# A two-layer streaming encoder on one core: the last stage's buffers split over two pools, the first opened earlier, and two scheduling orders dropped

## The chip, the cores and the metric

The kernel runs on one core of one Trainium2 chip. The metric is the device time of one execution, in microseconds (us). A core has TensorE (PE in the profile), VectorE (DVE), ScalarE (ACT), GpSimd (POOL) and SyncE (SP). Here nearly all transfers are issued from SP's queue, a few from ACT's. Each engine carries out its own instructions in program order and waits on semaphores for those of others.

## The reference

`x` is 1024 x 1024 float32 (frames by features). Two layers with residuals, each `x + mixer(rmsnorm(x))`, then a last rmsnorm. Layer 0:

```python
u_s5, g_s5, q, k, v, g_ret = split(h @ w_in)
y = gelu(s5_scan(u_s5))                       # diagonal state space, chunks of 64 frames
y_s5 = y * sigmoid(y @ glu_w + glu_b) * silu(g_s5)
q, k = rope(q) * 64**-0.5, rope(k)            # 8 heads, 64 wide; v 128 wide
y_ret = retention(q, k, v) * silu(g_ret)      # scores within chunks, a decayed state across
x = x + concat(y_s5, y_ret) @ w_out
```

Layer 1 is a Conformer convolution: `a, b, g = split(h @ w_in)`, `a * sigmoid(b)`, a causal depthwise convolution 31 frames wide, a layer norm, silu, a gate `silu(g)`, and an output projection.

## The kernel before

**Products.** A float32 operand is held as two halves that TensorE takes in a fast format: `h` (the value rounded) and `l` (value minus `h`). Each product is three matmuls, `h*h`, `h*l`, `l*h`. A `CAST` that makes an `h` and a subtraction that makes an `l` therefore stand ahead of every operand. Weights come by `wload_pieces` (`wf_X` from memory, `wh_X` on ACT, `wl_X` on POOL).

**Stages.** In time: projections and scan of layer 0 (to about 315 us), retention in four pairs of heads (pair 0 to 3, to about 545 us), the GLU product `y @ glu_w` (`mm_glu`, about 528 to 620 us, so it begins inside pair 3), the output projection, layer 1.

**Retention, one pair.** `ret_proj` makes q and k (`mm_q`, `mm_k`; `qraw` and `kraw` are evicted copies, `qswp` and `kswp` their halves swapped by small DMAs, `qrot` and `krot` the rotated results). Rope's table for q, 1 MB, comes as `ropeq_<pair>`. `ret_heads` makes transposed keys `kt` (from PE's `ktp`), the state products `kv` and the states `S`, the scores (`sp` on PE, masked on DVE into `sc`), and the outputs `ro`; then a norm and a gate `grl_<head>`, stored to memory as `yr_d`.

**y_pass.** In each pair two row blocks of the scan's output, `cb = k` and `k + 4`, are loaded (`yp_<cb>` from `y_d`), passed through gelu on ACT into `yn_<cb>` and stored to `yn_d`. DVE then makes four sums and differences of the two blocks (the GLU product is done with seven products of quarter size instead of eight) and splits the results: `th0_k` and `th1_k` are the `h` parts, `yn` is overwritten by the `l` part, and both are stored to `t_d`. The function is a generator; the caller runs it part by part (`next(parts)`). The pool tags `yp` (one buffer, shared by `yp_*` and `th*`) and `ynt` (two buffers) lie in pool `retq`, with rope's tables, `qraw`, `gs` and others. In pair 2 the store of `yn_6` goes out on ACT's queue; all other stores of this kind are on SP's.

**GLU operands.** `y_quarter` loads quarters of `yn_d` (`y11f`, `y21f`, `y22f`) and splits them. `load_split` reads quarters of `t_d` (`yt1h`, `yt2h`, ...). `gated` loads `yg` and `yn<nb>_<h>` (nb 0 to 3) for the gate behind the product, in pool `l1`; `gu` are copies of partial products. `gs`, stored to `ws_d`, are sums of the GLU's weights for the seven products.

**Order.** A scheduler simulates the kernel's instructions and writes each engine's order. It is steered by priorities, by buffers becoming free, by `issue_after(x)` (what is inside comes after x) and by `self.order(late, first)` (late is placed after first, where the engine would otherwise be free to choose). A pool's space is reused only when the earlier pool is closed; `early.close()` closes `retq` and pool `l1` (all of the last stage's buffers) is opened in its place. In pair 3, `turned()` is called behind the code for q's last addition (`qadds`, the sum that makes `qrot`).

Of the kernel before, what the change touches and what calls it, by code (L numbers as in the profile page):

```python
# [19 lines left out]
P = 128  # L20
# [51 lines left out]
class Trunk:  # L72
# [898 lines left out]
    def y_pass(self, rp, k):  # L971


        nc = self.nc
        yns = []
        for i, cb in enumerate((k, k + 4)):
            yt = rp.tile([P, 8, P], F32, name=f"yp_{cb}", tag="yp", bufs=1)
            self.wdma[f"yp{cb}"] = nc.sync.dma_start(yt[:], self.y_d[cb].rearrange("i h g m -> (h g) i m"))
            yn = rp.tile([P, P, 8], F32, name=f"yn_{cb}", tag="ynt", bufs=2)

            behind = {(2, 0): self.third_v, (2, 1): self.last_v, (3, 1): self.third_v}.get((k, i)) if k > 1 else None
            with self.tc.issue_after(behind.ins) if behind else nullcontext():
                nc.scalar.activation(yn[:], yt[:].rearrange("p i m -> p m i"), AF.Gelu_apprx_tanh)
            yn = yn[:].rearrange("p m i -> p (m i)")
            (nc.scalar if (k, i) == (2, 1) else nc.sync).dma_start(self.yn_d[cb * P:(cb + 1) * P], yn)
            yns.append(yn)
        (b11, b12), (b21, b22) = ((y[:, :HALF], y[:, HALF:]) for y in yns)
        v = nc.vector
        yield
        with self.tc.issue_after(self.last_raw.ins):  # L990
            v.tensor_tensor(b22, b22, b12, op=ALU.subtract)
            v.tensor_tensor(b12, b12, b11, op=ALU.subtract)
            v.tensor_tensor(b11, b22, b11, op=ALU.add)
            v.tensor_tensor(b21, b11, b21, op=ALU.subtract)
        yield
        for i in range(2):
            hi = rp.tile([P, T], F32R, name=f"th{i}_{k}", tag="yp", bufs=1)
            v.tensor_copy(hi[:], yns[i])
            if (k, i) == (1, 0):
                yield  # L1000
            v.tensor_tensor(yns[i].bitcast(F32R), yns[i], hi[:].bitcast(F32), op=ALU.subtract)
            self.wdma[f"th{i}_{k}"] = nc.sync.dma_start(self.t_d[i, 0, k * P:(k + 1) * P], hi[:].bitcast(F32))
            nc.sync.dma_start(self.t_d[i, 1, k * P:(k + 1) * P], yns[i])

    def glu_sums(self, g, tag):
# [5 lines left out]
        for i in range(2):  # L1011
            nc.sync.dma_start(q[i], self.A["w_glu"][i, m, :, :, c].rearrange("p j k n -> p j (k n)"))
        (a11, a12), (a21, a22) = ((t[:, 0, :], t[:, 1, :]) for t in q)
# [6 lines left out]
        with self.tc.issue_after(self.last_swap.ins):  # L1020
            for i in range(2):
                nc.sync.dma_start(self.ws_d[i, m, :, :, c].rearrange("p j k n -> p j (k n)"), q[i])

    def retention(self, st):
        nc, A = self.nc, self.A
        rp = self.rp = self.pool("ret", 1, stack=st)
        early = ExitStack()
        rq = self.rq = self.pool("retq", 1, stack=early, side="right")
        self.rk = rq.tile([P, 2, T], F32, name="ropek")
        nc.sync.dma_start(self.rk[:], A["rope_k"])  # L1030
# [3 lines left out]
        for pair in range(4):  # L1034
# [145 lines left out]
    def ret_heads(self, pair, K, Q, qadds, mask, kdec, V, turned, scored):  # L1180
# [12 lines left out]

        with self.tc.issue_after(self.last_kt.ins):
            for add in qadds:
                add()
# [113 lines left out]
    def layer0_back_and_layer1(self, st):  # L1310
# [55 lines left out]
        def gated(nb, h, z, turned=False):  # L1366
            yg = lp.tile([P, HALF], F32, name=f"yg{nb}_{h}", tag="u", bufs=5)
            nc.sync.dma_start(yg[:], self.gs_d[rows(nb), hs(h)])
            yn = lp.tile([P, HALF], F32, name=f"yn{nb}_{h}", tag="ev", bufs=3)
            nc.sync.dma_start(yn[:], self.yn_d[rows(nb), hs(h)])  # L1370
            times = lambda: gp.tensor_tensor(yg[:], yg[:], yn[:], op=ALU.mult)
# [632 lines left out]
```

## Time and profile before

| | |
|---|---|
| runs | 1134.13, 1137.13, 1139.33 us; median 1137.13 us |
| profiled execution | 1139.25 us, span 1137.5 us |
| busy | PE 1121.5 us (99%), DVE 854.2, POOL 645.7, ACT 496.3 |
| granted TensorE clock | near full in 39 of 40 slices |
| memory traffic | 261.46 MB, 230 GB/s mean |

The profile is that of one execution. Span is first to last instruction; what lies around it is 1139.25 - 1137.5 = 1.75 us. PE's busy time counts pipelined matmuls, so a 99% busy PE may still be slowed by short waits and by its clock. A row such as `484.38 2.07 PE L1254 MATMUL ro<-S,qrot ... x14 [3.06 <-DVE sc L1231]` says: 14 instructions from 484.38 us on, together 2.07 us, ahead of which PE stood idle for 3.06 us, ended by DVE's `sc` of line 1231.

### The profile page before, as it was taken

Reading aid. Unit: us, or ns where it says so; the run is one execution under the profiler, and the core shown is the slowest. Engines: PE = TensorE matmul, PEld = TensorE weight load, DVE = VectorE, ACT = ScalarE, POOL = GpSimd, SP = SyncE. Lnnn points to the kernel's source line nnn. Section 1 sums busy time; section 2 is a strip of 40 time slices with the busy share of each in tenths; the row PEclk is TensorE's granted clock in tenths of the full one; section 3 lists DMA queues with packets and bytes.
Section 4 is the critical chain, followed back from the end, with each engine's and each line's share of the span. In section 5 each row is a group of like instructions: output and inputs, shape, how many; then the busy total and the mean of one; then the engine's idle time right before and its main releaser. Section 6 shows DMA issues by size and latency. Waiting matters only on the chain.

```text
span 1137.5 us, 17227 instructions
## 1 busy us (share of the span) xinstructions
PE 1121.5 (99%) x6286; PEld 982.4 (86%) x6286; DVE 854.2 (75%) x1473; ACT 496.3 (44%) x729; POOL 645.7 (57%) x440
## 2 busy tenths in 40 slices
PE   9999999999999999999999999999999999999997
PEld 8888888888888889889888888888888888888876
DVE  7975798888418468476779633599999899999754
ACT  7323232232232231324446524546535676346673
POOL 2059999999246264341541110589544468678843
PEclk9999999999999999989999999999999999999999
DMA  9444365455397776767999988666678655358964
GB/s 346 131 140 145 116 207 179 172 175 182 114 305 280 246 225 199 273 208 256 379 367 320 357 317 279 204 221 205 239 254 295 237 183 173 112 171 265 320 229 167
DMA packets 118069, 261.46 MB, mean 230 GB/s; under 512 B 10720, under 2 KB 42464, under 8 KB 117344
## 3 DMA queue, kind: packets, MB, share of 16 engines
q1 hardware_dynamic: 114240, 247.22, 64.2%
q10 hardware_dynamic: 3744, 13.14, 3.0%
q8 instruction: 49, 0.80, 0.3%
q14 instruction: 36, 0.29, 0.1%
HBM read 181.48 MB, written 74.65 MB: 225 GB/s over the span
## 4 chain that ended last, share of the span: by engine, by line
PE 71%; DMA 9%; DVE 7%; POOL 6%; issue 3%; ACT 3%; SPq 1%; POOLq 0%; ACTq 0%; DVEq 0%
PE mm_g L213 10%; PE mm_wo L213 9%; PE mm_g L210 5%; PE mm_b L213 5%; PE mm_wo L210 5%; PE mm_a L213 5%; PE mm_u L213 3%; PE mm_oc L213 3%; PE mm_b L210 2%; PE mm_a L210 2%; PE mm_q L213 2%; PE mm_k L213 2%; PE mm_u L210 2%; PE y L962 1%; PE mm_oc L210 1%
## 5 line engine op out<-in xcount | busy, mean ns | idle before, releaser
L1604 DVE SCALAR_TENSOR_TENSOR cv<-u,convw,cv 128x512 f32<-128x512 f32 x390 | 268.3, 749 | 10.6 <-ACT cv L1570 8.5
L1564 POOL TENSOR_TENSOR tp<-tp,tp 128x512 f32<-128x512 f32 x64 | 83.0, 1297 | 33.8 <-ACT tp L1563 32.8
L210 PE MATMUL mm_g<-xh,wh_g 128*128 128x512 f32 x256 | 98.9, 386 | 0.0
L213 PE MATMUL mm_g<-xl,wh_g 128*128 128x512 f32 x256 | 97.3, 380 | 0.0
L213 PE MATMUL mm_g<-xh,wl_g 128*128 128x512 f32 x256 | 97.2, 380 | 0.0
L454 POOL TENSOR_TENSOR s1q<-s1q,s1q 128x512 f32<-128x512 f32 x12 | 17.6, 1465 | 89.8 <-ACT s1q L449 89.8
L1563 ACT ACTIVATE tp<-u,convw 128x512 f32<-128x512 f32 x64 | 45.4, 718 | 33.6 <-POOL tp L1564 32.7
L200 POOL TENSOR_TENSOR wl_glu<-wf_glu,wh_glu 128x1024 fp32r<-128x1024 f32 x14 | 34.3, 2455 | 42.1 <-ACT wh_glu L197 37.8
L210 PEld LDWEIGHTS mm_g<-xh,wh_g 128*128 128x128 f32 x256 | 48.4, 189 | 8.6 <-issue 1.2
L213 PEld LDWEIGHTS mm_g<-xh,wl_g 128*128 128x128 f32 x256 | 48.4, 189 | 6.9
L213 PEld LDWEIGHTS mm_g<-xl,wh_g 128*128 128x128 f32 x256 | 48.4, 189 | 6.7 <-issue 0.4
L200 POOL TENSOR_TENSOR wl_v<-wf_v,wh_v 128x1024 fp32r<-128x1024 f32 x12 | 31.3, 2608 | 37.2 <-ACT wh_v L197 37.1
L210 PE MATMUL mm_oc<-zh,wh_woc 128*128 128x512 f32 (+1 forms) x144 | 51.0, 365 | 1.2 <-ACT zh L1306 1.1
L213 PE MATMUL mm_oc<-zh,wl_woc 128*128 128x512 f32 (+1 forms) x144 | 51.3, 357 | 0.5 <-POOL wl_woc L200 0.5
L213 PE MATMUL mm_oc<-zl,wh_woc 128*128 128x512 f32 (+1 forms) x144 | 51.3, 357 | 0.0
L210 PE MATMUL mm_g<-h1h,wh_cg 128*128 128x512 f32 x128 | 48.9, 382 | 0.0
L210 PE MATMUL mm_wo<-ysh,wh_wos 128*128 128x512 f32 x128 | 48.9, 382 | 0.0
L213 PE MATMUL mm_b<-h1l,wh_cb 128*128 128x512 f32 x128 | 48.7, 381 | 0.1
L213 PE MATMUL mm_u<-xl,wh_u 128*128 128x512 f32 x128 | 48.6, 380 | 0.0
L213 PE MATMUL mm_b<-h1h,wl_cb 128*128 128x512 f32 x128 | 48.6, 380 | 0.0
L213 PE MATMUL mm_wo<-ysl,wh_wos 128*128 128x512 f32 x128 | 48.5, 379 | 0.0
L213 PE MATMUL mm_wo<-ysh,wl_wos 128*128 128x512 f32 x128 | 48.5, 379 | 0.0
(538 smaller groups left out, 3622.5 us busy)
## 6 DMA issues: line engine op xcount, KB each, us to landing
wf_g<-w_ab SPq DMA_DIRECT2D x16, 512.0 KB
wf_wos<-w_out SPq DMA_DIRECT2D x16, 512.0 KB
wf_wor<-w_out SPq DMA_DIRECT2D x16, 512.0 KB
wf_cb<-w_c SPq DMA_DIRECT2D x16, 512.0 KB
wf_ca<-w_c SPq DMA_DIRECT2D x16, 512.0 KB
wf_woc<-w_out_c SPq DMA_DIRECT2D x16, 512.0 KB
wf_v<-w_v SPq DMA_DIRECT2D x12, 512.0 KB
wf_cg<-w_c SPq DMA_DIRECT2D x11, 512.0 KB
```

The source lines that it names most:

```text
L200: self.low_made = self.lows[name] = lo[i].tensor_tensor(wl[:].rearrange(fl)[:, c], wf[:, c], h.bitcast(F32), op=ALU.subtract)
L210: nc.tensor.matmul(ps, wh[:, kb, :], xh, start=start, stop=False, **more)
L213: self.last_mm = nc.tensor.matmul(ps, a[:, kb, :], b, start=False, stop=stop and i == 1, **more)
L454: nc.gpsimd.tensor_tensor(a, a, sq[:], op=ALU.add)
L962: yield nc.tensor.matmul(ps[g2][:, cols(q)], W3[r, c, q, :], S[r, c, q, :], start=False, stop=q == 3 and c == 1)
L1563: nc.scalar.mul(sk[:], u[:, k:k + HALF], cw[:, nb, k:k + 1])
L1564: gp.tensor_tensor(s0[:], s0[:], sk[:], op=ALU.add)
L1604: v.scalar_tensor_tensor(dst[:], *tap, accs_[i][:], op0=ALU.mult, op1=ALU.add)
```

## The change

No operation is added or removed; every engine has as many instructions as before. What changes is where buffers lie and what the scheduler may put where:

1. `yp`, `ynt` and `th` move from `retq` into a pool of their own, `rety`.
2. In pair 3, `turned()` closes `retq` directly behind q's last addition and opens pool `l1a` in its place (tags `u`, `ev`, `tp`, `cq`, `cs`, `pilot`, `sq`; `yg` is tag `u`, `yn<nb>_<h>` tag `ev`). Then `y_pass`'s last part is run, `rety` closed and pool `l1b` opened for the other tags. Class `Two` picks the pool by tag.
3. In pair 3 q's last addition is no longer held behind `kt`, and y's last split (`th0_3`, `th1_3`) no longer behind the last of the `y11l` splits. Instead the first `y11l` split is put after `th0_3`'s low part.
4. Of five hand-made orders of DMAs four go: `y212` after `th0_3`, `yt200` after `th0_3`, `ropeq3` after `yp6`, `grl5` after `glu1`. The one of `yt100` after `glu9` stays.

```diff
+class Two:
+    FIRST = ("u", "ev", "tp", "cq", "cs", "pilot", "sq")
...
+    def tile(self, *args, tag=None, **kw):
+        pool = self.first if tag in self.FIRST else self.rest
+        return pool.tile(*args, **kw, **({"tag": tag} if tag else {}))
...
-            v.tensor_tensor(yns[i].bitcast(F32R), yns[i], hi[:].bitcast(F32), op=ALU.subtract)
+            low = v.tensor_tensor(yns[i].bitcast(F32R), yns[i], hi[:].bitcast(F32), op=ALU.subtract)
+            if (k, i) == (3, 0):
+                self.order(self.y_first, low)
...
         rq = self.rq = self.pool("retq", 1, stack=early, side="right")
+        sums = ExitStack()
+        ry = self.pool("rety", 1, stack=sums)
...
-                parts = self.y_pass(rq, pair)
+                parts = self.y_pass(ry, pair)
...
             def turned():
                 if pair == 3:
-                    with self.tc.issue_after(self.y_low.ins):
-                        next(parts, None)
                     early.close()
-                    self.lp = self.pool("l1", side="right")
+                    first = self.pool("l1a", side="right")
+                    next(parts, None)
+                    sums.close()
+                    self.lp = Two(first, self.pool("l1b", side="right"))
...
-        with self.tc.issue_after(self.last_kt.ins):
+        with self.tc.issue_after(self.last_kt.ins) if pair < 3 else nullcontext():
             for add in qadds:
                 add()
         turned()
...
+            if i == 0:
+                self.y_first = self.y_low
...
-        for late, first in (('y212', 'th0_3'), ('yt200', 'th0_3'), ('ropeq3', 'yp6'), ('grl5', 'glu1'), ('yt100', 'glu9')):
+        for late, first in (('yt100', 'glu9'),):
             self.order(self.wdma[late], self.wdma[first])
```

The remaining edits only store handles of DMAs in `wdma`. Lines of the changed file are 13 to 20 higher than before.

What it does to the order of instructions is seen at three places. First SP's queue between pairs 2 and 3. The rows before, from the load of weight `gs1_3` on:

```order
L1012 DMA gs1_3_4388<-w_glu 128x2x512
L1022 DMA ws_d_110<-gs1_3_4388 256x1x512
L985 DMA yn_d_91<-yn_2_4620 128x1024
L1288 DMA yr_d_92<-grl_3_4162 128x1024
L978 DMA yp_6_4623<-y_d_87 128x8x128
L1288 DMA yr_d_92<-grl_2_4160 128x1024
L1086 DMA ropeq_3_4845<-rope_q 128x2048
L1022 DMA ws_d_110<-gs0_3_4387 256x1x512
L1242 DMA grl_4_4695<-gr_d_90 128x1024
L193 DMA wf_glu0_4987<-w_glu 128x1024
L193 DMA wf_glu1_4993<-w_glu 128x1024
L1242 DMA grl_5_4697<-gr_d_90 128x1024
```

and after:

```order
L1027 DMA gs1_3_4391<-w_glu 128x2x512
L1104 DMA ropeq_3_4848<-rope_q 128x2048
L1037 DMA ws_d_110<-gs1_3_4391 256x1x512
L998 DMA yn_d_91<-yn_2_4623 128x1024
L1306 DMA yr_d_92<-grl_3_4165 128x1024
L991 DMA yp_6_4626<-y_d_87 128x8x128
L1306 DMA yr_d_92<-grl_2_4163 128x1024
L1037 DMA ws_d_110<-gs0_3_4390 256x1x512
L1260 DMA grl_4_4698<-gr_d_90 128x1024
L1260 DMA grl_5_4700<-gr_d_90 128x1024
L206 DMA wf_glu0_4990<-w_glu 128x1024
L206 DMA wf_glu1_4996<-w_glu 128x1024
```

`ropeq_3` has moved from behind the second `yr_d` store to directly behind `gs1_3`, and `grl_5` from behind the two `wf_glu` loads to in front of them.

The second place is SP's queue in pair 3, from the store of `yn_7` on. Before:

```order
L985 DMA yn_d_91<-yn_7_5215 128x1024
L1298 DMA y21f0_5473<-yn_d_91 128x512 x2
L1298 DMA y21f2_5484<-yn_d_91 128x512
L1002 DMA t_d_93<-th0_3_5259 128x1024
L1298 DMA y21f2_5484<-yn_d_91 128x512
L1343 DMA yt2h0_5511<-t_d_93 128x512
L1003 DMA t_d_93<-yn_3_5210 128x1024
```

and after:

```order
L998 DMA yn_d_91<-yn_7_5218 128x1024
L1388 DMA yg0_0_5578<-gs_d_89 128x512
L1390 DMA yn0_0_5580<-yn_d_91 128x512
L1390 DMA yn1_0_5605<-yn_d_91 128x512
L1390 DMA yn2_0_5679<-yn_d_91 128x512
L1345 DMA y22f0_5853<-yn_d_91 128x512
L1345 DMA y22f1_5859<-yn_d_91 128x512
L1345 DMA y22f2_5865<-yn_d_91 128x512
L1390 DMA yn3_0_5703<-yn_d_91 128x512
L1017 DMA t_d_93<-th0_3_5266 128x1024
L1018 DMA t_d_93<-yn_3_5213 128x1024
L1316 DMA y21f0_5480<-yn_d_91 128x512 x2
```

Eight loads of 256 KB, which were issued later before, now stand between the store of `yn_7` and that of `th0_3`; the four `y21f` loads come behind the stores of `th0_3` and its low part. `yn3_0` waits for a buffer of `yn0_0`, which POOL's product of `yg0_0` and `yn0_0` frees.

The third place is DVE at the same time (`CAST th` makes an `h` part, the row below it the low part). Before:

```order
L991 TENSOR_TENSOR yn_7_5215<-yn_7_5215,yn_3_5210 128x512
...
L1308 TENSOR_TENSOR y11l0_5225<-y11f0_5222,y11h0_5224 128x512
L1308 TENSOR_TENSOR y11l1_5230<-y11f0_5222,y11h1_5229 128x512
L1308 TENSOR_TENSOR y11l2_5236<-y11f2_5233,y11h2_5235 128x512
L1308 TENSOR_TENSOR y11l3_5241<-y11f2_5233,y11h3_5240 128x512
L998 CAST th0_3_5259<-yn_3_5210 128x1024
L1001 TENSOR_TENSOR yn_3_5210<-yn_3_5210,th0_3_5259 128x1024
L1191 TENSOR_TENSOR kt_3_5244<-ktp0_3_5245,kdec_3_4843 128x512
L1191 TENSOR_TENSOR kt_3_5244<-ktp1_3_5251,kdec_3_4843 128x512
L1112 TENSOR_TENSOR qrot_3_4978<-qrot_3_4978,qswp_3_4977 128x512 x2
L998 CAST th1_3_5264<-yn_7_5215 128x1024
```

and after:

```order
L1130 TENSOR_TENSOR qrot_3_4981<-qrot_3_4981,qswp_3_4980 128x512 x2
L1004 TENSOR_TENSOR yn_7_5218<-yn_7_5218,yn_3_5213 128x512
...
L1011 CAST th0_3_5266<-yn_3_5213 128x1024
L1014 TENSOR_TENSOR yn_3_5213<-yn_3_5213,th0_3_5266 128x1024
L1328 TENSOR_TENSOR y11l0_5228<-y11f0_5225,y11h0_5227 128x512
L1328 TENSOR_TENSOR y11l1_5233<-y11f0_5225,y11h1_5232 128x512
L1328 TENSOR_TENSOR y11l2_5239<-y11f2_5236,y11h2_5238 128x512
L1328 TENSOR_TENSOR y11l3_5244<-y11f2_5236,y11h3_5243 128x512
L1011 CAST th1_3_5271<-yn_7_5218 128x1024
L1014 TENSOR_TENSOR yn_7_5218<-yn_7_5218,th1_3_5271 128x1024
L1209 TENSOR_TENSOR kt_3_5247<-ktp0_3_5248,kdec_3_4846 128x512
L1209 TENSOR_TENSOR kt_3_5247<-ktp1_3_5254,kdec_3_4846 128x512
```

`qrot_3` is now ahead of y's four sums, `th0_3` and its low part ahead of the `y11l` splits, and `kt` behind `th1_3` and its low part.

More of the change, by code (lines that the diff above doesn't have):

```diff
@@ L58, with __init__ @@
 V_NG0, V_NG1, V_FG, V_GLUB, V_CB, V_LNG, V_LNB = range(7)
+class Two:
+    FIRST = ("u", "ev", "tp", "cq", "cs", "pilot", "sq")
+    def __init__(self, first, rest):
+        self.first, self.rest = first, rest
+    def tile(self, *args, tag=None, **kw):
+        pool = self.first if tag in self.FIRST else self.rest
+        return pool.tile(*args, **kw, **({"tag": tag} if tag else {}))
 class Halves:
@@ L984, in y_pass @@
             yn = yn[:].rearrange("p m i -> p (m i)")
-            (nc.scalar if (k, i) == (2, 1) else nc.sync).dma_start(self.yn_d[cb * P:(cb + 1) * P], yn)
+            self.wdma[f"y{cb}"] = (nc.scalar if (k, i) == (2, 1) else nc.sync).dma_start(self.yn_d[cb * P:(cb + 1) * P], yn)
             yns.append(yn)
@@ L1000, in y_pass @@
                 yield
[L1001 removed]
+            low = v.tensor_tensor(yns[i].bitcast(F32R), yns[i], hi[:].bitcast(F32), op=ALU.subtract)
+            if (k, i) == (3, 0):
+                self.order(self.y_first, low)
             self.wdma[f"th{i}_{k}"] = nc.sync.dma_start(self.t_d[i, 0, k * P:(k + 1) * P], hi[:].bitcast(F32))
[L1003 removed]
+            self.wdma[f"tl{i}_{k}"] = nc.sync.dma_start(self.t_d[i, 1, k * P:(k + 1) * P], yns[i])
     def glu_sums(self, g, tag):
@@ L1011, in glu_sums @@
         for i in range(2):
-            nc.sync.dma_start(q[i], self.A["w_glu"][i, m, :, :, c].rearrange("p j k n -> p j (k n)"))
+            self.wdma[f"gs{i}_{g}"] = nc.sync.dma_start(q[i], self.A["w_glu"][i, m, :, :, c].rearrange("p j k n -> p j (k n)"))
         (a11, a12), (a21, a22) = ((t[:, 0, :], t[:, 1, :]) for t in q)
@@ L1021, in glu_sums @@
             for i in range(2):
-                nc.sync.dma_start(self.ws_d[i, m, :, :, c].rearrange("p j k n -> p j (k n)"), q[i])
+                self.wdma[f"ws{i}_{g}"] = nc.sync.dma_start(self.ws_d[i, m, :, :, c].rearrange("p j k n -> p j (k n)"), q[i])
     def retention(self, st):
@@ L1367, in gated @@
             yg = lp.tile([P, HALF], F32, name=f"yg{nb}_{h}", tag="u", bufs=5)
-            nc.sync.dma_start(yg[:], self.gs_d[rows(nb), hs(h)])
+            self.wdma[f"yg{nb}_{h}"] = nc.sync.dma_start(yg[:], self.gs_d[rows(nb), hs(h)])
             yn = lp.tile([P, HALF], F32, name=f"yn{nb}_{h}", tag="ev", bufs=3)
-            nc.sync.dma_start(yn[:], self.yn_d[rows(nb), hs(h)])
+            self.wdma[f"yn{nb}_{h}"] = nc.sync.dma_start(yn[:], self.yn_d[rows(nb), hs(h)])
             times = lambda: gp.tensor_tensor(yg[:], yg[:], yn[:], op=ALU.mult)
```

2 lines of the change are left out of this document (1 added, 1 removed).

## The prediction

> **What bounds the kernel now.** First the page for the busy shares: PE carries the kernel from end to end, so only three things can move the time: PE's waits, its clock, and an operand that becomes late. I read PE's waits next (which line stood, who released it, us in total, times, longest):
>
> ```profile
> PEclk9999999999999999989999999999999999999999
> PE ro L1254 <- DVE sc L1231: 3.1, 1, 3.1
> PE mm_glu L210 <- ACT wh_glu L197: 1.4, 1, 1.4
> ...
> PE mm_glu L210 <- DVE mm_gluz L1447: 0.6, 1, 0.6
> ```
>
> The longest wait of all, 3.1 us on `ro`, lies where the change moves SP's queue, the second and the 0.6 us one in the GLU stage behind the other moves; and the one slice with a clock digit below 9 holds the first of them. So I read the chain that ended that wait, PE's timeline around it with the same stage of the next pair beside it, and three short windows (PE, PEld, DVE, ACT, POOL busy, clock, DMA share, GB/s):
>
> ```profile
> 464.18 6.71 DMA yp<-y_d
> ...
> 473.01 7.06 DMA yn_d<-yn
> ...
> 480.77 0.68 DVE kraw L1096
> ...
> 482.09 1.63 DVE yn L993
> ```
> ```profile
> 484.38 2.07 PE L1254 MATMUL ro<-S,qrot 64*128 64x128 f32 x14 [3.06 <-DVE sc L1231]
> 486.38 3.78 PE L1259 MATMUL ro<-v,sc 128*128 128x128 f32 x16
> 489.81 0.75 PE L210 MATMUL mm_k<-xh,wh_k 128*128 128x512 f32 x1
> 490.38 0.40 PE L213 MATMUL mm_k<-xl,wh_k 128*128 128x512 f32 x1
> ...
> 540.69 1.16 PE L1254 MATMUL ro<-S,qrot 64*128 64x128 f32 x16
> 541.78 2.05 PE L1259 MATMUL ro<-v,sc 128*128 128x128 f32 x16
> 543.59 0.46 PE L210 MATMUL mm_glu<-y21h,wh_glu 128*128 128x512 f32 x1
> ```
> ```profile
> 460.00:462.00 2.00, 2.00 (x20) 2.00 (x19) 1.56 (x4) 0.47 (x1) 0.00 (x0) 1.00 0.01 2
> 476.00:478.00 2.00, 2.00 (x22) 1.59 (x22) 0.85 (x2) 0.00 (x0) 0.35 (x1) 1.00 1.02 410
> 484.00:486.00 2.00, 1.62 (x13) 1.62 (x14) 2.00 (x4) 0.00 (x0) 0.00 (x0) 0.50 0.00 0
> 556.00:558.00 2.00, 1.52 (x7) 1.22 (x8) 2.00 (x5) 1.58 (x3) 1.88 (x2) 1.00 1.04 390
> ```
>
> The chain reads: `yp_6` is loaded, gelu makes `yn_6`, its store (on ACT's queue) starts at 473.01 and takes 7.06 us; only then may DVE overwrite `yn_6` with y's sums, and behind those stands `sc`, for which PE waits until 484.38. Behind the wait the clock is 0.50: the 14 + 16 `ro` matmuls up to 489.81 take 5.43 us, while the 32 of pair 3 take 543.59 - 540.69 = 2.90 us at full clock, that is 2.72 for 30. The wait has a second bill, about 5.43 - 2.72 = 2.7 us, and 490.38 - 489.81 = 0.57 instead of 0.22 us for the first `mm_k`, so 2.9 us in round numbers. Behind the 1.4 us wait (window 556 to 558) the clock stayed at 1.00. And the DMA engines, full at 410 GB/s while the store waits its turn, moved 2 GB/s at 460 to 462.
>
> **The change part by part.**
>
> *Rope's table for pair 3 goes ahead, `grl_5` too.* The issues and what they wait for:
>
> ```profile
> 456.42 0.63 SPq L1012 DMA_DIRECT2D gs<-w_glu  x1
> 462.01 0.59 SPq L1022 DMA_DIRECT2D ws_d<-gs  x1
> ...
> 466.90 0.51 SPq L1086 DMA_DIRECT2D ropeq<-rope_q  x1
> ...
> 469.73 6.99 SPq L193 DMA_DIRECT2D wf_glu<-w_glu  x2
> 476.83 0.36 SPq L1242 DMA_DIRECT2D grl<-gr_d  x1
> ```
> ```profile
> 456.49 2.52 POOL L1111 TENSOR_TENSOR qswp<-qswp,ropeq 128x512 f32<-128x512 f32 x2 [7.34 <-DMA qswp<-qraw]
> ```
>
> `ropeq_3` is now next after the load at 456.42, but its buffer is free only when POOL has read the old table, at 456.49 + 2.52 = 459.0. SP stands there from 457.1 until 459.0; the next row behind it was issued only at 462.0, so this wait delays nobody. The transfer of 1 MB then runs from 459.0 to about 461.6 (at 410 GB/s) in a stretch with idle DMA engines, instead of among the transfers in front of the `yn_6` store: 2.6 us of their work is gone. Against it, `grl_5` (0.5 MB, 1.3 us at that rate) now is ahead of the `wf_glu` loads, so among those in front. If the store comes out behind everything issued earlier it lands 1.3 us sooner with `grl_5` fully counted, 2.6 without. Bounds: 0 (the store on its own queue never waited for SP's) and 2.6. I take 1.8, between the two cases. Every us goes through: sums, `sc`, `ro` hang on that store. *First term: -1.8.* What is late next is `kraw`, which DVE does between the sums; it needs only `mm_k`, done before the wait.
>
> *The clock.* The wait then is 3.06 - 1.8 = 1.3 us, about as long as the 1.4 us behind which the clock stayed at 1.00. I take the half clock as gone: *second term: -2.9.* Bounds 0 and -2.9; the nearest row is the 1.4 us wait.
>
> [...]
>
> *Eight loads of 256 KB go ahead in pair 3; `y21f` and the stores of `th0_3` follow.* The stage in two windows, then the rows of SP and DVE:
>
> ```profile
> 520.00:530.00 10.00, 10.00 (x85) 9.82 (x84) 8.75 (x13) 5.82 (x11) 2.35 (x1) 1.00 0.43 128
> 530.00:540.00 10.00, 10.00 (x101) 8.56 (x100) 8.63 (x17) 2.23 (x4) 0.07 (x1) 1.00 1.01 338
> ```
> ```profile
> 516.86 0.32 SPq L985 DMA_DIRECT2D yn_d<-yn  x1
> ...
> 526.61 0.32 SPq L1002 DMA_DIRECT2D t_d<-th  x1
> ```
> ```profile
> 520.70 0.69 DVE L991 TENSOR_TENSOR yn<-yn,yn 128x512 f32<-128x512 f32 x1 [11.01 <-ACT v L1146]
> ...
> 523.48 2.50 DVE L1308 TENSOR_TENSOR y11l<-y11f,y11h 128x512 fp32r<-128x512 f32 x4
> ...
> 526.61 1.23 DVE L1001 TENSOR_TENSOR yn<-yn,th 128x1024 fp32r<-128x1024 f32 x1
> 528.26 1.29 DVE L1191 TENSOR_TENSOR kt<-ktp,kdec 128x512 f32<-128x512 f32 x2 [0.42 <-PE ktp L1189]
> ...
> 532.02 0.69 DVE L998 CAST th<-yn 128x1024 fp32r<-128x1024 f32 x1 [0.80 <-DMA t_d<-th]
> ```
> ```profile
> 528.71 0.38 PE L213 MATMUL mm_glu<-y11l,wh_glu 128*128 128x512 f32 x1
> ...
> 533.12 1.75 PE L1208 MATMUL kv<-v,kt 128*64 128x128 f32 x28
> ```
>
> From 520 to 530 the DMA engines were busy 0.43 of the time, from 530 on always: 5.7 us of idle transfer time, room for the 2 MB that move ahead (5.2 us at 390 GB/s). Everything behind them, the weights `wf_glu` included, then comes some us earlier. What that is worth is read from the two waits.
>
> ```profile
> 551.84 1.05 ACT L197 CAST wh_glu<-wf_glu 128x1024 fp32r<-128x1024 f32 x1 [0.80 <-DMA wf_glu<-w_glu]
> ...
> 554.83 0.67 ACT L1382 ACTIVATE sg<-mm_glu,hgb 128x512 f32<-128x512 f32 x1
> 555.40 1.03 ACT L197 CAST wh_glu<-wf_glu 128x1024 fp32r<-128x1024 f32 x1
> ```
> ```profile
> 588.08 1.05 ACT L197 CAST wh_glu<-wf_glu 128x1024 fp32r<-128x1024 f32 x1 [6.38 <-DMA wf_glu<-ws_d]
> ```
>
> The 1.4 us wait at 556.5 is for the `wh_glu` cast at 555.40, which ACT reached late: 0.80 us because it stood for a load at 551.84, and 0.57 us for the second `sg` ahead of it, which now is behind it. Together 1.37; I take *third term: -1.2*, bounds 0 (the load is not earlier) and -1.4. At 588.08 ACT again stood for a weight load, for 6.38 us, and DVE's `mm_gluz`, for which PE waits 0.6 us, is at the end of that chain. *Fourth term: -0.8*: the 0.6 us and as much again in the small delays of matmuls around it, cut by half; bounds 0 and -1.7.
>
> What these moves put at risk, each with its cover:
> - `y11l` comes behind `th0_3` and its low part, 0.69 + 1.23 = 1.9 us later, done at 527.9 instead of 526.0. PE takes the first at 528.71: cover 0.8 us, cost 0. Without it, PE's `mm_glu` waits as much.
> - `kt` now comes behind `th1_3`, which waits for the store of `th0_3` (they share a buffer). SP issues that store behind `yn3_0`, and `yn3_0` behind POOL's product. A 512 KB store out of a quiet stretch took 520.70 - 516.86 = 3.8 us, so `yg0_0` and `yn0_0` are there by about 522, POOL's product (2.52 / 2 = 1.3 us each for that size) by 523.4. `th0_3` is cast by 524.2 (the sums start at 520.70 as before and take 2.8 us). Issued at 524.3 its store lands between 528.1 (3.8 us) and 529.7 (5.4 us, as 526.61 to 532.02); then 0.69 + 1.23 + 1.29 us make `kt` at 531.3 to 532.9. PE wants it at 533.12: cover 0.2 to 1.8 us, cost 0.
> - `qrot` ahead of the sums falls into DVE's 11.01 us of idle time. Cost 0.
> - `y21f` is issued behind the stores of `th0_3`, some 2 us later, and ACT's casts come with it; PE takes the first `y21h` only at 543.59, some 15 us after those loads can land. Cost 0.
> - The pools only fix addresses; tags in `l1b` come free at the same event as before. Cost 0.
>
> *Sum:* -1.8 - 2.9 - 1.2 - 0.8 = -6.7 us, against the profiled execution's 1139.25: 1132.55. That execution is 2.1 us above the median of the runs shown (1137.13), which gives 1130.4. Since the terms lie nearer to their upper bounds than to 0, I take 1131.5.
>
> **The rivals.**
> - *The store does not care.* It is alone on ACT's queue, so it may have had its share of the engines whatever SP queued: `grl_5` and `wf_glu` still fill the engines when it comes. Then the first two terms are 0 and -2.0 is left: 1135.1. For it: the two queues are separate. Against it: 0.5 MB in 7.06 us is 74 GB/s out of 410, less than a fifth; a fair half would have been done in 2.6 us and a start.
>   [...]
> - *The clock halves all the same.* 1.3 us of waiting and what lies around it may be enough, or the wait shrinks by less. Then -1.8 - 2.0 = -3.8: 1133.3.
> - *The GLU stage gives its gain back.* Later `y21f`, ACT's other order, and a full DMA stretch that merely begins sooner: the third and fourth terms are 0: -4.7, 1132.4.
> - *Slower.* `th0_3`'s store is held up by `yn3_0`. If the eight loads slow one another and `yn0_0` lands as late as `yp` did in a full stretch (6.71 us), POOL is done at 525.9, the store lands at 529.7 to 531.3, `kt` is made at 532.9 to 534.5. Every us past 533.1 is one of PE's, with `kv`, `S` and `sc` behind it. It decides when the store lands after 529.9. At the worst the second cast stands as long again (some 4 us) and the wait of 3 to 4 us halves the clock as at 484: +3.9 + 2.9 = +6.8, with no gain in pair 2 to set against it 1143.9; with it (-4.7) about 1139.2.
>
> **How the numbers follow.** The forecast (both regions gain, full clock) has a chance of 0.47, the store's rival 0.14, the half clock 0.14, the GLU rival 0.12, the slower one 0.13. The range 1127.0 to 1138.0: below, all four terms at their bounds (-2.6 - 2.9 - 1.4 - 1.7 = -8.6 from the median: 1128.5) and 1.5 for the scatter of a median; above, the store's rival and the better part of the slower one. The likeliest case's own range is 1128 to 1133.5. What a measurement of this kernel can tell from no change is about 0.5%, 5.7 us: faster means under 1131.4, where somewhat over half of the forecast lies, with parts of the half clock's and the GLU rival's, and gains that I don't see: 0.42; slower (over 1142.8) only the worst end of the slower case: 0.08; the rest, 0.50, is no change that can be told.
>
> **What would show it.** In the changed kernel's trace: `ropeq` issued near 459 and the DMA engines busy from 459 to 462; the `yn_d` store on ACT's queue at 5 to 6 us instead of 7.06; the wait in front of `ro` at 1 to 1.5 us and no window at clock 0.50 around 485; DMA share well over 0.43 from 520 to 530; `th0_3`'s store issued by 524.5, `kt` ready ahead of PE's `kv`; no 1.4 us wait on `wh_glu`. The prediction is wrong if the store still takes 7 us, if a new wait of PE appears at `kv` or at `y11l`, or if the clock falls at another place.

## The result and the profile after

The changed kernel takes 1141.14 us (median of 14 runs, 1138.59 to 1144.31), the kernel before 1137.70 (14 runs, 1133.45 to 1140.74): ratio 1.0037, 95% interval 1.0025 to 1.0049. It is slower by some 4 us, where some 6 us faster (1131.5) was forecast. The profiled execution took 1141.18 us with a span of 1139.4, against 1139.25 and 1137.5 before. All rows below are of such single executions.

First PE's waits of the changed kernel, to be laid beside those that the prediction shows (line that stood, who released it, us in total, times, longest):

```profile
PE ro L1272 <- DVE sc L1249: 2.4, 1, 2.4
PE mm_glu L223 <- ACT sg L1402: 1.9, 1, 1.9
PE mm_glu L223 <- ACT mm_glus L1402: 1.3, 1, 1.3
...
PE mm_glu L226 <- DVE y11l L1328: 0.4, 1, 0.4
```

The wait on `ro` has shrunk from 3.1 to 2.4 us, not to 1.3. The wait of 1.4 us in the GLU stage is now one of 1.9. The 0.6 us on `mm_gluz` are gone, and in their place stand 1.3 us on `mm_glus` and 0.4 on `y11l`.

Where the time goes is seen in PE's timeline at three milestones: the last `mm_q` of pair 3, the first matmul on `yt2`, the first `mm_wo` of the stage that follows. Before:

```profile
505.09 0.38 PE L213 MATMUL mm_q<-xh,wl_q 128*128 128x512 f32 x1
...
556.48 0.48 PE L210 MATMUL mm_glu<-yt2h,wh_glu 128*128 128x512 f32 x1 [1.41 <-ACT wh_glu L197]
...
613.28 0.38 PE L210 MATMUL mm_wo<-ysh,wh_wos 128*128 128x512 f32 x1
```

and after, with the two waits between:

```profile
484.38 2.07 PE L1272 MATMUL ro<-S,qrot 64*128 64x128 f32 x14 [2.36 <-DVE sc L1249]
...
505.33 0.38 PE L226 MATMUL mm_q<-xh,wl_q 128*128 128x512 f32 x1
...
530.85 0.48 PE L226 MATMUL mm_glu<-y11l,wh_glu 128*128 128x512 f32 x1 [0.44 <-DVE y11l L1328]
...
557.93 0.48 PE L223 MATMUL mm_glu<-yt2h,wh_glu 128*128 128x512 f32 x1 [1.92 <-ACT sg L1402]
559.58 0.63 PE L226 MATMUL mm_glu<-y21l,wh_glu 128*128 128x512 f32 x1
...
611.36 0.48 PE L223 MATMUL mm_glu<-yt1h,wh_glu 128*128 128x512 f32 x1 [1.34 <-ACT mm_glus L1402]
...
616.64 0.38 PE L223 MATMUL mm_wo<-ysh,wh_wos 128*128 128x512 f32 x1
```

`ro` starts at 484.38 in both kernels, and `mm_q` ends 0.24 us apart: between pairs 2 and 3 the change brought nothing. From there to `mm_wo` it was 613.28 - 505.09 = 108.19 us and is 616.64 - 505.33 = 111.31. The loss of 3.1 us lies in the GLU stage. The windows say why the matmuls around 559.58 take 0.63 us each (PE, PEld, DVE, ACT, POOL busy, clock, DMA share, GB/s):

```profile
484.00:486.00 2.00, 1.62 (x13) 1.62 (x14) 2.00 (x4) 0.00 (x0) 0.00 (x0) 0.52 0.00 0
520.00:530.00 10.00, 10.00 (x86) 9.87 (x86) 8.89 (x9) 5.01 (x9) 3.47 (x2) 1.00 0.88 304
555.00:560.00 5.00, 3.08 (x12) 2.19 (x11) 3.32 (x7) 4.78 (x7) 4.62 (x3) 0.92 0.36 121
558.00:562.00 4.00, 4.00 (x12) 3.17 (x13) 1.79 (x4) 1.79 (x3) 4.00 (x4) 0.65 0.87 275
```

The clock is still halved at 484 to 486 and now also behind the 1.92 us wait: the 4 us at 0.65 lose 4 x 0.35 = 1.4 us, and since it is at 0.50 from 559.16 to 562.57, 3.41 us, it is 1.7 us in all. The account of the stage is then 0.44 (`y11l`) + 0.51 (1.92 for 1.41) + 1.7 (clock) + 1.34 (at 611) - 0.6 (the one gone) = 3.4 us, a little more than the 3.1 measured. Behind 616 the two executions differ by 1.4 us the other way, which is less than the runs of one kernel scatter. That the stage itself is longer is no accident of one execution: in the next part's two runs it is 608.66 - 502.61 = 106.05 us (e1, the kernel before but for two orders) and 613.80 - 502.09 = 111.71 us (e3, the changed kernel but for the same two).

The eight loads do fill the idle stretch (share 0.88 from 520 to 530, before 0.43). But the idle time comes back: 0.36 from 555 to 560, where before the engines were full. The bytes were moved, and the weights behind them came no sooner.

**Why PE waits at 558 and 611.** First the two weight loads on SP's queue before:

```profile
531.87 0.42 SPq L193 DMA_DIRECT2D wf_glu<-w_glu  x1
...
545.61 0.33 SPq L193 DMA_DIRECT2D wf_glu<-w_glu  x1
```

and SP's queue, then ACT and DVE, of the changed kernel:

```profile
525.02 0.32 SPq L1390 DMA_DIRECT2D yn<-yn_d  x1
525.58 0.32 SPq L1017 DMA_DIRECT2D t_d<-th  x1
...
531.42 0.32 SPq L1316 DMA_DIRECT2D y21f<-yn_d  x1
...
537.00 0.64 SPq L206 DMA_DIRECT2D wf_glu<-w_glu  x1
...
546.79 0.33 SPq L206 DMA_DIRECT2D wf_glu<-w_glu  x1
```
```profile
553.28 1.04 ACT L210 CAST wh_glu<-wf_glu 128x1024 fp32r<-128x1024 f32 x1 [2.65 <-DMA wf_glu<-w_glu]
...
556.27 1.03 ACT L210 CAST wh_glu<-wf_glu 128x1024 fp32r<-128x1024 f32 x1
557.20 0.68 ACT L1402 ACTIVATE sg<-mm_glu,hgb 128x512 f32<-128x512 f32 x1
...
590.50 0.62 ACT L1326 CAST y22h<-y22f 128x512 fp32r<-128x512 f32 x1 [2.88 <-DMA y22f<-yn_d]
```
```profile
591.16 0.69 DVE L1328 TENSOR_TENSOR y22l<-y22f,y22h 128x512 fp32r<-128x512 f32 x1 [3.72 <-ACT y22h L1326]
```

SP stands for POOL before `yn3_0` (525.02), then for a free `y21f` buffer (531.42). Behind that stand the weights: `wf_glu2` is issued at 537.00, where before it was 531.87. The wait at 558 hangs on the next one, `wf_glu3`: it is issued at 546.79 behind all eight `yt3` loads (2 MB), where before it was 545.61 behind seven of them, so of the 5.1 us only 1.2 are left there. ACT waits 2.65 us for that load where it had waited 0.80 (cast at 553.28, before 551.84), the next cast and `sg` follow, and PE stands until 557.93. At 590 ACT and DVE now take the split of `y22f3` ahead of the gate's work. Its load is late, DVE stands for 3.72 us and so begins the next `mm_gluy` at 591.77 instead of 586.21; it has little idle time after that (0.73 and 0.66 us up to 611), and a PSUM bank is emptied late for PE at 611.

### The profile page after: what moved, and what is told of

It is laid out like the page before. It is cut to its first block, busy times and chain, and to the rows that moved or that the text cites. A ratio compares the mean times of both kernels' runs of the same rounds, so it can differ in the third digit from the quotient of the medians.

```text
span 1139.4 us, 17220 instructions
## 1 busy us (share of the span) xinstructions
PE 1123.3 (99%) x6286; PEld 983.9 (86%) x6286; DVE 856.1 (75%) x1473; ACT 495.6 (43%) x729; POOL 644.2 (57%) x440
## 4 chain that ended last, share of the span: by engine, by line
PE 77%; DMA 7%; DVE 5%; POOL 5%; ACT 3%; issue 2%; SPq 0%; POOLq 0%; ACTq 0%; DVEq 0%
PE mm_g L226 10%; PE mm_wo L226 10%; PE mm_g L223 5%; PE mm_wo L223 5%; PE mm_b L226 5%; PE mm_a L226 5%; PE mm_u L226 3%; PE mm_oc L226 3%; PE mm_k L226 2%; PE mm_b L223 2%; PE mm_a L223 2%; PE mm_q L226 2%; PE mm_u L223 2%; PE y L975 1%; PE v L904 1%
## 5 line engine op out<-in xcount | busy, mean ns | idle before, releaser
L226 PE MATMUL mm_a<-h1h,wl_ca 128*128 128x512 f32 x128 | 48.6, 380 | 0.1
```

Of the source, the lines that this page charges most:

```text
L226: self.last_mm = nc.tensor.matmul(ps, a[:, kb, :], b, start=False, stop=stop and i == 1, **more)
```

## The experiments

In the lists below a pair such as `('ropeq3', 'yp6')` puts the first DMA behind the second. Each ratio is to 29 or 35 runs of the kernel before on the same chip, with its 95% interval in brackets; each experiment has 12 runs (e5 has 6) and one profiled execution.

### The two orders that the change drops: e1 and e3

e1 takes them out of the kernel before, e3 gives them back to the changed one.

```diff
 e1, in the kernel before
-        for late, first in (..., ('ropeq3', 'yp6'), ('grl5', 'glu1'), ('yt100', 'glu9')):
+        for late, first in (..., ('yt100', 'glu9')):
 e3, in the changed kernel
-        for late, first in (('yt100', 'glu9'),):
+        for late, first in (('ropeq3', 'yp6'), ('grl5', 'glu1'), ('yt100', 'glu9')):
```

> The kernel before, with only the two orders of ropeq3 and grl5 removed, so that SP's queue between pairs 2 and 3 stands as in the changed kernel and nothing else moves. Theory A (what rope's table saves the yn_6 store it costs the yp_6 load ahead of it): the yp_6 load takes 7.5 to 8 us instead of 6.7, the store 5 to 5.5 instead of 7.1, PE still waits 2.3 to 3.1 us for ro, the clock still halves behind it; time within 1.5 us of the kernel before. Theory B (the prediction's): wait 1.3 us, full clock, 4 to 5 us faster.

> The changed kernel with the two orders of ropeq3 and grl5 put back; only these two SP rows move. Theory A (the loss is all in the GLU stage): 0 to 1 us slower than the changed kernel, 3 to 4.5 us slower than before; PE's waits for mm_glu at 530, 556 and 610 stay. Theory D (the loss comes from the moves between pairs 2 and 3): back to the time of before.

Measured: e1 1.0006 [0.9990, 1.0021], as the kernel before; e3 1.0034 [1.0019, 1.0048], as the changed one. The two orders are worth nothing that can be told in time, and the loss is in the rest of the change. e1 was expected to have a store of 5 to 5.5 us; it took 7.35 us. e3's rows on PE, and a window behind the wait:

```profile
482.59 1.16 PE L1272 MATMUL ro<-S,qrot 64*128 64x128 f32 x14 [1.33 <-DVE sc L1249]
483.67 3.68 PE L1277 MATMUL ro<-v,sc 128*128 128x128 f32 x16
```
```profile
483.00:487.00 4.00, 4.00 (x27) 3.88 (x24) 4.00 (x15) 0.00 (x0) 0.00 (x0) 0.59 0.33 133
```

With the old order the wait is 1.33 us here, the size that I had forecast for the new one, and the clock falls all the same (0.59). The wait differs as much among kernels with one order: 3.1, 2.8 and 1.3 us in three with the old order, 1.1 to 4.1 in ten with the new one.

### Rope's table still later: e2 and e8

Both are the kernel before with `ropeq_3` behind another DMA, so that the store of `yn_6` has fewer transfers ahead of it.

```diff
-  ('ropeq3', 'yp6')
+  ('ropeq3', 'th0_2')   e2
+  ('ropeq3', 'glu1')    e8
```

> The kernel before with one SP row moved: ropeq_3 (1 MB) behind the store of th0_2 instead of behind yp_6, so that it is neither ahead of the yp_6 load nor ahead of the yn_6 store. Theory A: yp_6's load stays at 6.7 us, the yn_6 store falls from 7.1 to 4.5 to 5.5 us, PE's wait for ro falls from 3.1 to 0.5 to 1.3 us, and no half clock is left around 485: 4 to 5.5 us faster than before. Theory C (a store on ACT's own queue does not mind what SP has queued): store 7 us, wait 3 us, time as before.

> The kernel before with one SP row moved: ropeq_3 behind the two wf_glu loads, that is behind yp_6's load and issued after the yn_6 store has started, but 7 to 10 us earlier than in the run that put it behind th0_2. Theory A: the wait for ro between pairs 2 and 3 stays under 1 us and the clock full there, as in that run; the table is there in time, so no wait for y11l and none above 1.5 us near 556; 3 to 5 us faster than before. Rival: the table is still late for POOL's qrot, DVE's q and y sums follow late, and the gain is lost in the GLU stage again.

Measured: e2 1.0029 [1.0012, 1.0046], e8 1.0004 [0.9992, 1.0017]. Both take away the `ro` wait and its half clock (1.00 from 478 to 492 in e2, from 484 to 488 in e8); the store of `yn_6` takes 4.85 us in e2 and 4.40 in e8. e2 pays with a `y11l` wait of 4.5 us and a `wh_glu` wait of 2.9. e8 tells more; its PE rows and windows:

```profile
481.27 1.29 PE L1254 MATMUL ro<-S,qrot 64*128 64x128 f32 x16
...
484.29 0.46 PE L210 MATMUL mm_k<-xh,wh_k 128*128 128x512 f32 x1
...
554.42 0.80 PE L210 MATMUL mm_glu<-yt2h,wh_glu 128*128 128x512 f32 x1 [3.65 <-ACT wh_glu L197]
```
```profile
484.00:488.00 4.00, 4.00 (x22) 3.57 (x22) 4.00 (x20) 0.60 (x2) 0.00 (x0) 1.00 0.76 294
554.00:558.00 4.00, 3.58 (x9) 2.87 (x10) 3.10 (x7) 2.39 (x4) 3.63 (x3) 0.50 1.03 382
```

`mm_k` starts at 484.29 instead of 489.81: the 5.5 us that I had counted on are there, by another means. Yet at `yt2` PE waits 3.65 us for the same cast and the clock halves there: 554.42 instead of 556.48, and at `mm_wo` 0.8 us are left (612.45 for 613.28). PE was ready 4.3 us earlier (550.77 for 555.07), but ACT, which stood 4.23 us for the load of `wf_glu3`, made its cast only 2.1 us earlier (549.77 for 551.84). The weight came too late to pass the gain on, and it became a wait.

### The late weights: e4, e9 and e10

e4 puts `wf_glu2` ahead of the store of `th1_3`. e9 (kernel before) and e10 (changed kernel) put the `yt3` loads behind the weight that ACT waits for.

```diff
 e4, in the changed kernel
+  ('th1_3', 'glu2')
 e9, in the kernel before; e10, in the changed kernel
+  *((f"yt3{k}{j}", 'glu4') for k in range(4) for j in range(2))
```

> The changed kernel with one order added: the store of th1_3 behind the load wf_glu2, which moves wf_glu2 from 11 rows later than in the kernel before back to about its old place. Theory A (wf_glu2, held behind the stores of pair 3, delays the whole chain of load, cast on ACT, low part on POOL and the next load into the freed buffer): wf_glu2 issued near 532 instead of 537, the wait of mm_glu near 556 falls from 1.9 to 1.4 us or less and the half clock behind it goes; 2.5 to 4 us faster than the changed kernel, so within 1.5 us of before. Theory E (the loss is DVE's late y11l and kt, slowed by POOL): at most 0.7 us faster than the changed kernel.

> The kernel before with the eight yt3 loads (2 MB, not used until the product after yt2) put behind the weight loads wf_glu3 and wf_glu4 on SP. Theory W (the wait of mm_glu<-yt2h near 556 is a wall set by the stream of transfers from 525 on and the weight load at its end, not by PE): wf_glu3 lands 3 to 5 us sooner, the 1.4 us wait falls to 0.7 or less (ACT's norm rows then set it): 0.5 to 1.5 us faster than before. Rival: the wait is ACT's or POOL's own and stays.

> The changed kernel with wf_glu3 and wf_glu4 ahead of the yt3 loads; only SP rows move (and one POOL pair). Theory W: wf_glu3 lands before 550.6, the 1.9 us wait near 556 falls below 0.5 and the half clock behind it goes; the 1.3 us wait near 610 stays: 2.5 to 3.5 us faster than the changed kernel, level with before. Theory G or F (the loss is spread over DVE's order and the early loads): less than 1 us.

Measured: e4 1.0036 [1.0021, 1.0052]; it missed its aim, for `wf_glu2` was still issued only at 537.74, since SP stood ahead of it for the `y21f` buffers. e9 1.0004 [0.9993, 1.0015], no gain, where 0.5 to 1.5 us were expected: its wait at 556 is 0.5 us, but 1.0 us appears at `mm_wo`. e10 1.0022 [1.0011, 1.0032]. In e10's rows ACT has the weight in time, and PE no longer waits at `yt2`, nor does the clock fall (its `mm_glu` matmuls there take 0.38 to 0.48 us, where those of the changed kernel took up to 0.63):

```profile
551.70 1.03 ACT L210 CAST wh_glu<-wf_glu 128x1024 fp32r<-128x1024 f32 x1
...
555.61 0.68 ACT L1402 ACTIVATE sg<-mm_glu,hgb 128x512 f32<-128x512 f32 x1
```
```profile
PE mm_glu L223 <- ACT mm_glus L1402: 1.4, 1, 1.4
...
PE mm_wo L223 <- ACT yr0h L1326: 0.6, 1, 0.6
```

The stage is 109.3 us instead of 111.3, and the second wait, of 1.4 us, stands. By the ratios this is somewhat under half the loss (0.0015 of 0.0037), but e10's interval and that of the changed kernel overlap.

### Undoing single parts: e5, e6 and e13

e5 gives `y11l` its old place ahead of `th0_3` back, e6 puts seven of the eight loads behind the `yt3` loads again, e13 does both.

```diff
 e5 and e13, in the changed kernel
-            if (k, i) == (3, 0):
-                self.order(self.y_first, low)
...
-                    next(parts, None)
+                    with self.tc.issue_after(self.y_low.ins):
+                        next(parts, None)
 e6 and e13
+  *((n, 'yt321') for n in ('yg0_0', 'yn0_0', 'yn1_0', 'yn2_0', 'y220', 'y221', 'y222'))
```

> The changed kernel with y's last split put back behind the y11l splits on DVE (before's issue_after, without the order of the first y11l behind th0_3); the early loads, pools and SP's other moves stay. Theory F (th0_3 ahead of y11l is the root: the y11f buffers come free 5 us later, SP stands at the y21f loads, and wf_glu2 queued behind them is 5 us late): y11l done by 528 instead of 531.4, y21f's second pair issued by 528 instead of 531.4, wf_glu2 by 533 instead of 537; no wait of PE for y11l; the 1.9 us wait near 556 at 1.4 or less, no half clock there; the 1.3 us wait near 610 stays. 1.5 to 3 us faster than the changed kernel. Theory G (the eight early loads are the root): within 1 us of the changed kernel.

> The changed kernel with the eight early loads put back behind yt3's third load, about where they stood before; DVE's order (th0_3 first) stays. Theory F: DVE still splits th0_3 first, y11l is done near 529.5 (it still runs beside POOL's wl_glu1, but th0_3's cast no longer beside POOL's product), y21f's second pair is issued near 529.5 and the loss is half there: 0.5 to 1.5 us faster than the changed kernel, 2 to 3 us slower than before. Theory G (the early loads are the root): back to within 1 us of before.

> The changed kernel with both undone: y's last split behind the y11l splits, and the eight loads back at about their old place. Pools, qrot ahead of the sums and the dropped DMA orders stay. Theory J (each of the two is enough to lengthen the stage: th0_3 first delays y11l, the early loads bring POOL's product beside y11l and SP's stand): the stretch from the last mm_q to the first yt2 matmul falls from 52.6 to 51.4 us or less and that from there to the output projection from 58.7 to 57 or less; time within 1 us of before. Rival (qrot's place or the dropped orders): stays 3 us slower than before.

Measured: e5 1.0046 [1.0030, 1.0062], e6 1.0030 [1.0018, 1.0042], e13 1.0017 [1.0000, 1.0035]. Undoing either part alone gives no gain that can be told. e5 keeps the waits of 1.8 and 1.3 us, has one of 0.7 on `y11l`, and a new one of 2.0 us ahead of `sp`: its four `y11l` splits take 5.74 us, beside two rows of POOL, and what follows them on DVE is late. e6 loses the wait at 611 but has one of 3.8 us at `yt2`. e13 lies half way, its interval begins at 1.0000 and overlaps that of the changed kernel; it doesn't settle how the loss divides between the two parts.

### The split at 590, alone and with the weights: e7 and e14

e7 puts the last `y22` split behind the work of the gate at that place: ACT's cast behind the tanh, DVE's low part behind the gate's product. e14 does this and the `yt3` orders of e10.

```diff
+                    if (nb, h) == (5, 0):
+                        self.order(self.lastlow["y223"][0], tanh)
+                        self.order(self.lastlow["y223"][1], gate)
```

> The changed kernel with two orders added: the last y22 cast on ACT and its low part on DVE go behind the gate of the second mm_gluy, about where they stood before. Theory H (DVE stands 3.7 us for the last y22f load ahead of the first mm_gluy, and PE pays 1.3 us near 610 for a bank that ACT and DVE empty late): DVE has no such stand near 588, the 1.3 us wait near 610 falls below 0.4; 1 to 1.5 us faster than the changed kernel. Rival: the load is late anyway and the wait moves to the y22 matmuls; no gain.

> The changed kernel with wf_glu3 and wf_glu4 ahead of the yt3 loads and the last y22 split behind the second gate: the waits near 556 and near 610 cured together. If they carry the loss: last mm_q to yt2 50.6 us, yt2 to the output projection 55.5 us, 3 to 4 us faster than the changed kernel and level with before. If each cure is given back further on: 1 us or less beyond the run with the yt3 loads late alone, so 1.5 to 2.5 us slower than before.

Measured: e7 1.0035 [1.0019, 1.0051], e14 0.9991 [0.9976, 1.0005]. e14's interval and that of the changed kernel do not touch, and it isn't told apart from the kernel before: with both waits gone the loss is gone. The `yt3` order alone gave the kernel before nothing (e9), which speaks against a gain of another kind from that order. Its waits and two of the milestones:

```profile
PE ro L1272 <- DVE sc L1249: 3.1, 1, 3.1
...
PE mm_glu L226 <- DVE y11l L1328: 1.0, 1, 1.0
...
PE mm_wo L223 <- ACT yr0h L1326: 0.6, 1, 0.6
```
```profile
506.96 0.38 PE L226 MATMUL mm_q<-xh,wl_q 128*128 128x512 f32 x1
...
613.26 0.38 PE L223 MATMUL mm_wo<-ysh,wh_wos 128*128 128x512 f32 x1
```

The stage takes 613.26 - 506.96 = 106.3 us, 5.0 less than in the changed kernel; the ratios differ by 0.0046, or 5.2 us. The waits of 1.9 and 1.3 us are gone, while the `ro` wait of 3.1 us stands as it did before. That e7 alone gives nothing in time, though its profiled stage was 107.5 us, stays open. In that one execution, the second fastest of the twelve (1137.39 us of 1136.54 to 1146.54), the wait at 556 was 1.6 us and the clock held (1.00 from 555 to 563); that the clock falls there in others is my guess, not shown.

### Both regions at once: e11, e12 and e15

The rope order of e8 is added: to e9 (e11), to e10 (e12), to e14 (e15).

```diff
+  ('ropeq3', 'glu1'), ('grl5', 'glu1')
```

> The kernel before with both: ropeq_3 behind the wf_glu loads and the yt3 loads behind wf_glu4. Theory W: the 5 us that the former run gained between pairs 2 and 3 and lost again near 556 (a wait of 3.8 us and a half clock behind it) now stay: wait near 556 under 1 us, full clock there; 4 to 6 us faster than before. Rival (something else pins that place to the landing of y's sums): the wait stays over 2.5 us and the time as before.

> The changed kernel with the same two moves. Theory W: as the former, less the 1.3 us near 610 and the wait for y11l near 530: 3 to 5 us faster than the changed kernel with the yt3 loads late alone, 2 to 4 us faster than before.

> The same with ropeq_3 behind the wf_glu loads. The stretch up to mm_k of pair 3 is 4.5 us shorter, y's sums come 2.4 us later after the last mm_q, the rest as in the run before: 2 to 3 us faster than that run, 1.5 to 3 us faster than before. If there is a further wall: as the kernel before.

Measured: e11 0.9994 [0.9981, 1.0006], e12 1.0000 [0.9988, 1.0011], e15 0.9988 [0.9975, 1.0001]. e12 and e15 are faster than the changed kernel, and none of the three is told apart from the kernel before. `mm_k` starts 4.5 to 6.2 us earlier in each than in the kernel before, and each pays later: e11 with 1.1 us ahead of `sp` and 0.9, 0.8 and 0.7 us in the GLU stage, e12 with 2.7 us on `y11l` at 522 and 1.3 on `mm_glus`, e15 with 3.0 on `y11l` and 1.1 on `wl_wos`. The gains of 1.5 to 6 us that were expected over the kernel before did not come.

### Who slows `y11l`: e16

`y11l` was one of the covers that the prediction priced at 0. In the changed kernel its rows on DVE and POOL read:

```profile
523.77 1.78 DVE L1011 CAST th<-yn 128x1024 fp32r<-128x1024 f32 x1
526.73 4.67 DVE L1328 TENSOR_TENSOR y11l<-y11f,y11h 128x512 fp32r<-128x512 f32 x4
```
```profile
523.64 1.35 POOL L1391 TENSOR_TENSOR yg<-yg,yn 128x512 f32<-128x512 f32 x1 [6.27 <-DMA yn<-yn_d]
527.88 2.37 POOL L213 TENSOR_TENSOR wl_glu<-wf_glu,wh_glu 128x1024 fp32r<-128x1024 f32 x1 [2.88 <-ACT wh_glu L210]
```

Both DVE rows are long (0.68 for the cast and 2.50 for the four splits before), and beside each POOL is at work. e16 gives POOL's second row to DVE, later.

```diff
-  [self.nc.vector if name[:2] in LO_V or name[:3] in LO_V else self.nc.gpsimd]
+  [self.nc.vector if name[:2] in LO_V or name[:3] in LO_V or name == "glu1" else self.nc.gpsimd]
```

> The changed kernel with wl_glu1 (the low part of one weight block) made by DVE behind th1_3 instead of by POOL beside y11l. Theory K (DVE's SBUF-to-SBUF splits stand while POOL works on SBUF): the four y11l take 2.5 us instead of 4.7, done by 529.5; no wait of PE for y11l; th0_3's cast still takes 1.8 us (POOL's product is still beside it); kt about 1 us earlier. Time 0.5 to 1.5 us faster than the changed kernel. Rival (the 4.7 us are waits for ACT's casts or PE): y11l stays at 4.7.

e16's rows:

```profile
523.51 1.77 DVE L1011 CAST th<-yn 128x1024 fp32r<-128x1024 f32 x1
526.46 2.49 DVE L1328 TENSOR_TENSOR y11l<-y11f,y11h 128x512 fp32r<-128x512 f32 x4
```
```profile
523.45 1.28 POOL L1391 TENSOR_TENSOR yg<-yg,yn 128x512 f32<-128x512 f32 x1 [6.62 <-DMA yn<-yn_d]
```

With POOL's `wl_glu` gone from there the four splits take 2.49 us again; the cast, with POOL's product still beside it, keeps its 1.77. In both DVE lost a little less than what POOL worked in that time: 4.67 - 2.49 = 2.18 us beside 2.37, and 1.77 - 0.68 = 1.09 beside 1.28. The ratio is 1.0027 [1.0010, 1.0043], not told apart from the changed kernel's: the two other waits stay (2.6 and 1.4 us), so this stall is real and at most a small part of the loss.

## Why the prediction was wrong, point by point

In place of -1.8 - 2.9 - 1.2 - 0.8 = -6.7 us the four terms came out as 0, 0, +0.5 and +0.7, and two costs came that no term had: 1.7 of half clock in the GLU stage and 0.4 at `y11l`.

- **First term (-1.8), rope's table ahead.** `ropeq` was issued at 459.74, about as said, and the engines were no longer idle from 460 to 462 (153 GB/s for 2). But its transfer took 6.75 us, not 2.6, and ran into the load of `yp_6`: 7.88 us instead of 6.71. So gelu began at 472.81 instead of 470.97, and the store, itself faster (5.19 us for 7.06), was issued at 474.84 instead of 473.01. The changed kernel's rows on SP, ACT and DVE:

```profile
459.74 0.34 SPq L1104 DMA_DIRECT2D ropeq<-rope_q  x1
...
472.81 2.00 ACT L996 ACTIVATE yn<-yp 128x1024 f32<-128x1024 f32 x1 [4.97 <-DMA yp<-y_d]
474.84 0.33 ACTq L998 DMA_DIRECT2D yn_d<-yn  x1
...
480.16 0.69 DVE L1004 TENSOR_TENSOR yn<-yn,yn 128x512 f32<-128x512 f32 x1 [2.62 <-DMA yn_d<-yn]
```

  In the kernel before, the same sum also began at 480.16. The step that failed is "instead of among the transfers in front of the `yn_6` store": I gave a transfer that has the engines almost alone the 410 GB/s of a full stretch with many under way (1 MB in 6.75 us is some 155 GB/s), and did not count what it does to the load in front of that store. How the delay divides between load and store changes from kernel to kernel (7.32 and 7.35 us in e1, with the same order), but the two together take 13.1 to 15.7 us in the ten kernels with the table ahead and 13.8 to 14.2 in the three with the old order. The term is 0, and e1 and e3 show it in the times.
- **Second term (-2.9), the half clock.** It hung on the first one, and the wait was 2.36 us. The second step that failed is "about as long as the 1.4 us behind which the clock stayed at 1.00": e3 has a wait of 1.33 us and a clock of 0.59. One row of a wait without a fall of the clock was no threshold. The term is 0. (Its size was also added up short: 2.7 and 0.57 - 0.22 = 0.35 make 3.1, not 2.9.)
- **Third term (-1.2), the wait at 556.** The step that failed is "Everything behind them, the weights `wf_glu` included, then comes some us earlier". SP issues in the order of its queue, and the loads moved ahead brought two rows with them that wait for buffers. `wf_glu2` was issued 5.1 us later, and `wf_glu3`, for which ACT and then PE wait, 1.2 us later instead of some us earlier. That the buffers alone make up the 1.2 us is not shown, since e4 did not move `wf_glu2`; that PE's wait hangs on the place of `wf_glu3` is shown by e10. The term is +0.5, with 1.7 of half clock behind it, which no term had.
- **Fourth term (-0.8), the stage to 626.** The 0.6 us did go, but the early loads also moved the split of `y22` ahead of the gate, and a wait of 1.34 us came at 611 (in e6, with the loads late again, and in e7 and e14, with the split behind the gate, it is gone). I named no instruction of ACT or DVE at 590 as moved, though the order of both kernels had it. The term is +0.7.
- **The covers.** `y11l`: 0.8 us of cover were claimed and 0.44 us of wait came, since the four splits took 4.67 us beside POOL's row (2.49 in e16, without it). This wait and the half clock at 559 are two of the three things that the prediction had named as signs of being wrong. `kt` and `kv`: no wait at `kv`, as said. `th0_3`'s store was issued at 525.58, 1.1 us later than forecast.
- **The rivals.** *The store does not care* gave the first two terms right, but for another reason: the store does care (4.40 and 4.85 us in e8 and e2, with the table behind it, for 7.06), and with the table ahead the load in front of it pays. *Slower* named the right place, SP behind `yn3_0`, and the wrong victim: it is not `kt` but the weights that stand behind it in the queue. The range ended at 1138.0, since I let no case be slow in the GLU stage except by `kt`.

Three things of the change stay without a number of their own: the pools' new addresses and the new place of `qrot` were not tried apart, and e13 leaves the division between the early loads and the order of `y11l` open.

## What to carry to other kernels

When loads are moved ahead in a queue that is issued in order, follow the queue to the next weight and write down each buffer that a row in between waits for; idle transfer time ahead of a weight is no gain if the queue stands (here `wf_glu2` was issued 5.1 us later). Where the transfers are full, look for what they deliver last: TensorE, coming there earlier, only waited longer in e8 (3.65 us for 1.41) and paid with its clock (0.50 from 554 to 558). A gain of several us read from one wait should be tested against the next wait in the same execution, before it is counted.

## What the runs showed of the hardware

**DVE and POOL.** Four splits on DVE took 4.67 us beside a POOL row of 2.37 us and 2.49 us without it (e16): 4.67 - 2.49 = 2.18 us lost beside 2.37 us of POOL. The cast ahead of them took 1.78 us beside a POOL row of 1.35 us in the changed kernel, 1.77 us beside one of 1.28 us in e16, and 0.68 us in the kernel before, with no row of POOL beside it. Why DVE loses this time is not shown.

**The clock.** The length of a wait alone doesn't decide whether it halves: it did behind 1.33 us (e3), 1.6 (e1), 1.92 (the changed kernel) and 3.65 (e8), and did not behind 1.41 (the kernel before), 1.64 (e7), 1.8 and 2.0 (e5), nor behind the 2.7 us of e12. e12's window with that wait:

```profile
522.00:528.00 6.00, 3.27 (x17) 2.59 (x16) 5.96 (x7) 0.00 (x0) 2.47 (x1) 1.00 0.68 244
```

The clock column stays at 1.00 through a window in which PE was busy 3.27 us of 6. Between 440 and 630 us the half clocks were of two lengths: 3.41 us (559.16 to 562.57 in the changed kernel) and 6.83 us (484.07 to 490.89 there, 483.59 to 490.42 in the kernel before). Windows of 1 us give 3.4 us also for those of e1, e3, e7, e13, e14, e15 and e16, and 6.8 us for that of e10. The starts of the two in one execution lie 75.09 us apart in the changed kernel (484.07 and 559.16), that is 22 times 3.413, and 71.68 in e3 (483.70 and 555.38, from windows of 1 us), 21 times as much. What decides between a wait with a half clock and one without is not shown.
